# FFN of sub-blocks 1 to 3: the norm's sums of squares behind the first gate step, the spreading of its factors inside the first up step

## The chip, the cores and the metric

The kernel runs on one core of a Trainium2 chip. TensorE (PE, with its weight loads as PEld) multiplies, VectorE (DVE), ScalarE (ACT) and GpSimd (POOL) do the element work, and SyncE (SP) issues the transfers. Each engine works through its own list of instructions in order and waits on semaphores for the others. TensorE writes into PSUM, of which the kernel uses eight tiles of 128 x 512 numbers (called banks here): four for large products (the pool "acc") and four for everything else (the pool "mps").

The metric is the time of one execution on the device, in microseconds. All times below are microseconds.

## The reference

One layer of a hybrid decoder, on 2048 prompt tokens and 8 x 4 sample tokens: a mixer (gated linear attention and a spatial gating unit), attention over 256 memory tokens, and a gated MLP with a causal convolution of width 3 over the tokens. The change touches the way into the last of them:

```
def rmsnorm(x, g):
    xf = x.astype(jnp.float32)
    y = xf * lax.rsqrt(jnp.mean(xf * xf, axis=-1, keepdims=True) + EPS)
    return (y * g.astype(jnp.float32)).astype(x.dtype)

# the MLP, in words:
#   n  = rmsnorm(x, g_ffn)                 1024 columns
#   a  = causal_conv3(n @ w_gate) + bias   2816 columns
#   x += (gelu(a) * (n @ w_up)) @ w_down
```

The factor of the norm is one number for each token, so it can be multiplied in behind the product: `n @ w` is `(x * g) @ w` times that number. The kernel does that: its products start from `x * g`, and the factor comes in later, in g = q x factor (before the convolution) and once more behind the GELU for the up half.

## The kernel before, in words

**Tiling.** The prompt is worked through in four sub-blocks s = 0 to 3 of 512 tokens; in the FFN sub-block 2 also takes the 32 sample tokens (544 columns). Activations lie with features on partitions, tokens along the row. Every float32 product is three passes with rounded halves (`mm3`, lines 92 to 94: high x high, low x high, high x low); a matmul here is one such pass of 128 x 128 weights.

**The FFN.** 2816 columns are 22 tiles of 128, taken in pairs as 11 gate steps and 11 up steps that alternate (gate 0, up 0, gate 1, ...), with down steps woven in later. In sub-block 0 a step is an ordinary product with 512 tokens (`gate`, `upp`). In sub-blocks 1 to 3 it is `gate7` or `upp7`, which share `seven_step`: the 2 x 2 x 2 blocks of a step in seven products (A11, S1, A12, S2, S3, S4, A22) rather than eight, on half the tokens (256, or 272) each, from sums of token blocks (`w1`, `wu`, `wt`, `wb`, made by DVE and ACT for each pair of feature tiles, four pairs) and sums of weight tiles. A product is 4 pairs x 3 passes, 12 matmuls; a step is 84. For gate step 0 (`early`) all seven products first run over the three token pairs that are there, then over the last pair; its products A11, S1, A12 and S2 take the four banks of "acc", S3, S4 and A22 take banks of "mps". When a product is complete, DVE or ACT adds it to the step's result q (lines 266 to 288), and `use` consumes q.

**The norm.** The last product of the attention (`out_proj_steps`, product name wx) calls `finish(m)` for each of the eight feature tiles: ACT squares it, POOL adds the squares up in `wxsq` (line 1265). Two steps follow:

- `stat` (here called xstat, lines 1267 to 1277): matmuls of `wxsq` with a column of ones give the sum for each token in `wxss` (128 x 4, line 1272; a float32 matmul is two passes, so 8 in the profile, 10 in sub-block 2), DVE scales it into `rt` (line 305), POOL raises it to the power -1/2 (`wxrs`, line 306).
- `start` (fstart), that is `bcast_tokens` (lines 308 to 323): DVE makes four diagonal tiles `dg_f` (line 313), four matmuls with ones spread them over all partitions into the bank `bcp_f` (line 314), ACT copies it to `bc_f` (line 316); sub-block 2 has a small fifth one (`bcps_f`, lines 321 and 322).

`bc_f` is first read by the gate step's `use`: `gate_put` (line 1540) makes g = q x bc_f, and `conv` runs the convolution and the GELU.

**What sets the order.** The kernel is written as a list of steps, `x2 + [xstat, fstart] + fmain`, and a scheduler places the instructions of each engine from this list, by its own model of times and by what is free. A step written earlier has its PSUM bank reserved earlier, so wxss and bcp_f take banks of "mps" ahead of S3, S4 and A22 of gate step 0.

Of the kernel before, what the change touches and what calls it, by code (L numbers as in the profile page):

```python
# [37 lines left out]
def hymba_step_kernel(  # L38
# [172 lines left out]
            return wsplit(raw[:, :1024].rearrange("p (k m) -> p k m", k=8), name)  # L211
        return load

    def seven_step(plain, sums, get_xs, H, use, name, early=False):


        seq = ("A11", "S1", "A12", "S2", "S3", "S4", "A22") if early else ("A11", "S2", "S1", "S3", "A12", "S4", "A22")
# [14 lines left out]
        def fn(*ws):  # L232
# [6 lines left out]
            q = wraw(f"q_{name}")  # L239
# [3 lines left out]
            def prod(nm, k0, k1):  # L243
                if nm not in ps:
                    mate = {"S3": "S1", "A22": "S4"}.get(nm)
                    if joint and mate:
                        ps[nm] = ps[mate][0], 1
                    else:
                        ps[nm] = (mps if early and len(ps) > 3 else acc)(f"a_{name}{nm}"), 0
                bank, i = ps[nm]  # L250
                for k in range(k0, k1):
                    mm3(bank[:, i * H:(i + 1) * H], half(nm, 0, k), half(nm, 1, k), *xs[k][nm], k == 0, k == last)
# [9 lines left out]
                    prod(nm, 0, last)  # L262
            for nm in seq:
                prod(nm, last if early else 0, last + 1)
                if nm == "A11":
                    act.activation(q0, got(nm), AF.Copy)
                elif nm == "S2":
# [237 lines left out]
    w7d = {}  # L505
# [1012 lines left out]
    def ffn_steps(B, last=False):  # L1518
# [36 lines left out]
        def gate7(j):  # L1555
            f = 2 * j
            H = T // 2

            def use(*q):
                for i in range(2):  # L1560
                    cur["g", f + i] = gate_tile(f + i)
                    gate_put((dve, pool)[i], f + i, q[i], 0, T)
                    conv(f + i)
            return seven_step(*w7d["g", j], lambda: B.hn, H, use, f"wg{s}{j}", j == 0)

        def conv(f):
# [29 lines left out]
        def upp7(j):  # L1596
            f = 2 * j
            H = T // 2

            def use(*q):  # L1600
                for i in range(2):
                    c = cur[f + i]
                    (dve, pool)[i].tensor_tensor(c[:, :T], q[i], c[:, :T], ALU.mult)  # L1603
                    acts[f + i] = (U(f"acth{s}{f + i}", F32R), U(f"actl{s}{f + i}", F32R))
                    split(acts[f + i][0][:, :T], acts[f + i][1][:, :T], c[:, :T])
            return seven_step(*w7d["u", j], lambda: B.hn, H, use, f"wup{s}{j}")

        def turn_h(j):

# [147 lines left out]
    for s, B in enumerate(blocks):  # L1757
# [18 lines left out]
        steps += w2 + [stat, scales]  # L1776
        steps += weave(sc + x1, (turns[:2], 8, 9), (turns[2:3], 13, 13), (turns[3:], 14, 14))
        fstart, fmain, flast = ffn_steps(B, s == NSB - 1)
        steps += x2 + [xstat, fstart]
        sides = []  # L1780
        if B.mix_sample:
            sides.append((sample_steps(), 1, len(fmain) - 5))
# [46 lines left out]
```

## Time and profile before

| | |
|---|---|
| time, median of 3 runs (lowest, highest) | 2842.79 (2840.3, 2844.05) |
| span of the profiled execution | 2835.0 |
| TensorE busy, share of the span | 2794.4, 99% |
| weight loads busy | 2473.9, 87% |
| DVE, ACT, POOL busy | 1891.3, 1104.5, 575.5 |
| first gate matmul of sub-block 1, 2, 3 | 1120.12, 1810.65, 2476.49 |

The profile is of one execution; times in it count from its start. A row of its timeline gives start, duration, engine, line, operation and tiles (out<-in), with the number of instructions drawn together as x, and in brackets the idle time of the engine just before and what ended it. Tile names lose their numbers where rows are grouped (a_wg30S stands for the sums S1 to S4 of gate step 0 of sub-block 3, a_wg30A for A11, A12, A22). TensorE's durations overlap: the distance from start to start is what a matmul costs.

### The profile page before, as it was taken

What the parts mean: (1) busy time and instruction counts of PE and PEld (TensorE: products, weight loads), DVE (VectorE), ACT (ScalarE), POOL (GpSimd) and SP (SyncE); (2) the same over time, 40 slices, a digit from 0 to 9 for tenths busy, and PEclk for the clock granted to TensorE, in tenths of its full rate; (3) what the DMA queues carried; (4) which work ended last, traced back from release to release, by engine and by line L of the source; (5) the groups of instructions that cost most, each with busy time, mean ns of one, the idle gap of its engine ahead of it and who ended that gap; (6) DMA issues with size and microseconds to landing.
All of it is one profiled execution on the core that took longest, in us unless ns stands there. A gap on an engine that the chain in (4) does not pass through costs nothing.

```text
span 2835.0 us, 47063 instructions
## 1 busy us (share of the span) xinstructions
PE 2794.4 (99%) x17894; PEld 2473.9 (87%) x17894; DVE 1891.3 (67%) x3266; ACT 1104.5 (39%) x1950; POOL 575.5 (20%) x638
## 2 busy tenths in 40 slices
PE   8999999999999999999999999999999999999998
PEld 8888888888888898898888889899999888899997
DVE  6578778777657776655555777766666677665555
ACT  5645544333363354222124445422223545421222
POOL 2002212111111221222220121222221022132222
PEclk9999999999999999999999999999999999999999
DMA  9756589999932255888995226577776323577775
GB/s 306 244 182 219 188 273 340 335 339 333 328 109 77 83 164 196 309 290 290 324 340 169 82 61 208 196 260 256 258 264 215 102 70 133 201 260 273 271 282 177
DMA packets 369687, 638.21 MB, mean 225 GB/s; under 512 B 27370, under 2 KB 238412, under 8 KB 369462
## 3 DMA queue, kind: packets, MB, share of 16 engines
q1 hardware_dynamic: 369462, 635.20, 65.9%
q8 instruction: 142, 2.33, 0.3%
q14 instruction: 83, 0.68, 0.1%
HBM read 507.69 MB, written 127.41 MB: 224 GB/s over the span
## 4 chain that ended last, share of the span: by engine, by line
PE 61%; DVE 4%; ACT 1%; issue 1%; POOL 1%; DMA 0%; POOLq 0%; SPq 0%; DVEq 0%; ACTq 0%
PE d L94 4%; PE d L92 4%; PE d L93 4%; PE a_wx L94 1%; PE a_wx L93 1%; PE a_wx L92 1%; PE s L1044 1%; PE a_wo L92 1%; PE a_wo L93 1%; PE a_wu L92 1%; PE a_wu L93 1%; PE a_wo L94 1%; PE t_wr L92 1%; PE t_wr L93 1%; PE a_wu L94 1%
## 5 line engine op out<-in xcount | busy, mean ns | idle before, releaser
L92 PE MATMUL d<-acth,whi_wd 128*128 128x272 f32 (+1 forms) x688 | 235.3, 342 | 0.0
L94 PE MATMUL d<-acth,wlo_wd 128*128 128x272 f32 (+1 forms) x688 | 233.3, 340 | 0.0
L93 PE MATMUL d<-actl,whi_wd 128*128 128x272 f32 (+1 forms) x688 | 233.0, 339 | 0.0
L1679 DVE TENSOR_TENSOR h<-d,h 128x512 f32<-128x512 f32 (+1 forms) x232 | 133.5, 581 | 148.0 <-PE d L94 147.8
L1581 POOL TENSOR_TENSOR c<-c,bc_f 128x512 f32<-128x512 f32 (+1 forms) x88 | 139.3, 1589 | 134.2 <-ACT c L1580 133.4
L1571 ACT ACTIVATE c<-g,colsb 128x512 f32<-128x512 f32 x88 | 71.7, 815 | 202.9 <-DVE g L1540 152.7
L94 PEld LDWEIGHTS d<-acth,wlo_wd 128*128 128x128 f32 x688 | 129.3, 188 | 15.5 <-issue 1.2
L93 PEld LDWEIGHTS d<-actl,whi_wd 128*128 128x128 f32 x688 | 129.3, 188 | 13.6 <-issue 0.4
L92 PEld LDWEIGHTS d<-acth,whi_wd 128*128 128x128 f32 x688 | 129.5, 188 | 13.1
L1603 POOL TENSOR_TENSOR c<-r_q_wup,c 128x512 f32<-128x512 f32 (+1 forms) x33 | 63.0, 1908 | 337.7 <-DVE r_q_wup L286 215.9
L1568 POOL COPY carry<-g 128x2 f32<-128x2 f32 x88 | 30.6, 348 | 432.8 <-DVE g L1540 430.7
L92 PE MATMUL a_wo<-ch,h_wo 128*128 128x512 f32 (+1 forms) x320 | 113.2, 365 | 2.3 <-ACT r L874 1.5
L93 PE MATMUL a_wo<-cl,h_wo 128*128 128x512 f32 (+1 forms) x320 | 113.4, 357 | 0.0
L94 PE MATMUL a_wo<-ch,l_wo 128*128 128x512 f32 (+1 forms) x320 | 112.6, 355 | 0.0
L1572 DVE SCALAR_TENSOR_TENSOR c<-g,colsb,c 128x512 f32<-128x512 f32 x88 | 86.0, 978 | 29.0 <-ACT c L1571 28.3
L84 ACT ACTIVATE acth<-c 128x512 fp32r<-128x512 f32 (+1 forms) x88 | 55.9, 636 | 117.1 <-DVE c L1603 87.3
L94 PE MATMUL a_wx<-pTh,wlo_wx 128*128 128x512 f32 x256 | 101.2, 395 | 0.0
L93 PE MATMUL a_wx<-pTl,whi_wx 128*128 128x512 f32 x256 | 100.5, 393 | 0.0
L92 PE MATMUL a_wx<-pTh,whi_wx 128*128 128x512 f32 x256 | 100.2, 394 | 0.0
L1580 ACT ACTIVATE c<-c 128x512 f32<-128x512 f32 (+1 forms) x88 | 56.1, 637 | 96.6 <-DVE c L1573 84.7
L1573 DVE SCALAR_TENSOR_TENSOR c<-g,colsb,c 128x512 f32<-128x512 f32 x88 | 88.0, 1000 | 1.1
L85 DVE TENSOR_TENSOR actl<-c,acth 128x512 fp32r<-128x512 f32 (+1 forms) x88 | 64.2, 733 | 27.2 <-ACT acth L84 26.2
(3753 smaller groups left out, 9725.5 us busy)
## 6 DMA issues: line engine op xcount, KB each, us to landing
whi_wd<-wd SPq DMA_DIRECT2D x66, 512.0 KB, 7.8
wlo_wd<-wd SPq DMA_DIRECT2D x66, 512.0 KB, 7.5
r_wo<-in_w_out_dram SPq DMA_DIRECT2D x32, 512.0 KB, 3.5
wlo_wx<-vod SPq DMA_DIRECT2D x32, 512.0 KB, 4.1
whi_wx<-vod SPq DMA_DIRECT2D x32, 512.0 KB, 4.8
r_wg<-in_w_gate_dram SPq DMA_DIRECT2D x22, 512.0 KB, 7.4
r_wup<-in_w_up_dram SPq DMA_DIRECT2D x22, 512.0 KB, 4.7
r_wd<-in_w_down_dram SPq DMA_DIRECT2D x22, 512.0 KB, 4.3
```

What stands on the lines that cost most here:

```text
L84: act.activation(hi, src, AF.Copy)
L85: (lo_eng or dve).tensor_tensor(lo, src, hi.bitcast(F32), ALU.subtract)
L92: pe.matmul(ps, wh, xh, start=first, stop=False)
L93: pe.matmul(ps, wh, xl, start=False, stop=False)
L94: pe.matmul(ps, wl, xh, start=False, stop=last)
L1571: act.activation(c[:, :SB], g[:, 2:SB + 2], AF.Identity, bias=cb, scale=w2)
L1572: dve.scalar_tensor_tensor(c[:, :SB], g[:, 1:SB + 1], w1, c[:, :SB], ALU.mult, ALU.add)
L1573: dve.scalar_tensor_tensor(c[:, :SB], g[:, 0:SB], w0, c[:, :SB], ALU.mult, ALU.add)
L1580: act.activation(c[:, :T], c[:, :T], AF.Gelu_apprx_tanh)
L1581: pool.tensor_tensor(c[:, :T], c[:, :T], B.fbc[:, :T], ALU.mult)
L1603: (dve, pool)[i].tensor_tensor(c[:, :T], q[i], c[:, :T], ALU.mult)
L1679: dve.tensor_tensor(B.h[m + mm][:, cs], ps[:, :cw], B.h[m + mm][:, cs], ALU.add)
```

## The change

For sub-blocks 1 to 3 the two steps leave the list. The first gate step's `use`, called when its seven products have been written, runs xstat in place of its own work and keeps its results q; the first up step gets a function `then`, which `seven_step` calls behind product S1: it runs `start` (the spreading) and then the gate's real `use` with the kept results. Sub-block 0 is as before, since its steps aren't of this form. No instruction is added or taken away.

```diff
--- before.py
+++ after.py
@@ -211,7 +211,7 @@
             return wsplit(raw[:, :1024].rearrange("p (k m) -> p k m", k=8), name)
         return load
 
-    def seven_step(plain, sums, get_xs, H, use, name, early=False):
+    def seven_step(plain, sums, get_xs, H, use, name, early=False, then=None):
 
 
         seq = ("A11", "S1", "A12", "S2", "S3", "S4", "A22") if early else ("A11", "S2", "S1", "S3", "A12", "S4", "A22")
@@ -262,6 +262,8 @@
                     prod(nm, 0, last)
             for nm in seq:
                 prod(nm, last if early else 0, last + 1)
+                if then and nm == "S1":
+                    then()
                 if nm == "A11":
                     act.activation(q0, got(nm), AF.Copy)
                 elif nm == "S2":
@@ -1557,10 +1559,16 @@
             H = T // 2
 
             def use(*q):
+                if j == 0 and "late" not in cur:
+                    B.xstat()
+                    cur["late"] = q
+                    return
                 for i in range(2):
                     cur["g", f + i] = gate_tile(f + i)
                     gate_put((dve, pool)[i], f + i, q[i], 0, T)
                     conv(f + i)
+            if j == 0:
+                cur["use"] = use
             return seven_step(*w7d["g", j], lambda: B.hn, H, use, f"wg{s}{j}", j == 0)
 
         def conv(f):
@@ -1603,7 +1611,12 @@
                     (dve, pool)[i].tensor_tensor(c[:, :T], q[i], c[:, :T], ALU.mult)
                     acts[f + i] = (U(f"acth{s}{f + i}", F32R), U(f"actl{s}{f + i}", F32R))
                     split(acts[f + i][0][:, :T], acts[f + i][1][:, :T], c[:, :T])
-            return seven_step(*w7d["u", j], lambda: B.hn, H, use, f"wup{s}{j}")
+            def then():
+                start()
+                cur.pop("use")(*cur["late"])
+                del cur["late"]
+
+            return seven_step(*w7d["u", j], lambda: B.hn, H, use, f"wup{s}{j}", then=then if j == 0 else None)
 
         def turn_h(j):
 
@@ -1776,7 +1789,8 @@
         steps += w2 + [stat, scales]
         steps += weave(sc + x1, (turns[:2], 8, 9), (turns[2:3], 13, 13), (turns[3:], 14, 14))
         fstart, fmain, flast = ffn_steps(B, s == NSB - 1)
-        steps += x2 + [xstat, fstart]
+        B.xstat = xstat.fn
+        steps += x2 + ([xstat, fstart] if s == 0 else [])
         sides = []
         if B.mix_sample:
             sides.append((sample_steps(), 1, len(fmain) - 5))
```

**TensorE, end of gate step 0 of sub-block 3.** Before (a_wg30S2 is product S2, its operands the token sums wu, the last pair with the number 37; wup30A11 is the up step's first product):

```order
L93 MATMUL a_wg30A11_25852<-w1wx37_25789,wg30A11_25566 128x256
L94 MATMUL a_wg30A11_25852<-w1wx37_25789,wg30A11_25566 128x256
L92 MATMUL a_wg30A12_25872<-wbhwx37_25798,wg30A12_25627 128x256
L93 MATMUL a_wg30A12_25872<-wblwx37_25799,wg30A12_25627 128x256
L94 MATMUL a_wg30A12_25872<-wbhwx37_25798,wg30A12_25627 128x256
L1272 MATMUL wxss3_25811<-ones_86,wxsq3_25525 128x1 x4
L92 MATMUL a_wg30S2_25882<-wuhwx37_25802,wg30S2_25629 128x256
L92 MATMUL a_wup30A11_25988<-w1wx31_25544,wup30A11_25720 128x256
L93 MATMUL a_wup30A11_25988<-w1wx31_25544,wup30A11_25720 128x256
L94 MATMUL a_wup30A11_25988<-w1wx31_25544,wup30A11_25720 128x256
```

And now:

```order
L93 MATMUL a_wg30S4_25878<-wblwx37_25799,wg30S4_25659 128x256
L94 MATMUL a_wg30S4_25878<-wbhwx37_25798,wg30S4_25659 128x256
L93 MATMUL a_wg30S1_25838<-wtlwx37_25794,wg30S1_25568 128x256
L94 MATMUL a_wg30S1_25838<-wthwx37_25793,wg30S1_25568 128x256
L93 MATMUL a_wg30S3_25868<-wtlwx37_25794,wg30S3_25657 128x256
L94 MATMUL a_wg30S3_25868<-wthwx37_25793,wg30S3_25657 128x256
L92 MATMUL a_wg30A22_25888<-wuhwx37_25802,wg30A22_25718 128x256
L93 MATMUL a_wg30A22_25888<-wulwx37_25803,wg30A22_25718 128x256
L94 MATMUL a_wg30A22_25888<-wuhwx37_25802,wg30A22_25718 128x256
L1274 MATMUL wxss3_25927<-ones_86,wxsq3_25525 128x1 x4
L92 MATMUL a_wup30A11_25953<-w1wx31_25544,wup30A11_25720 128x256
L93 MATMUL a_wup30A11_25953<-w1wx31_25544,wup30A11_25720 128x256
```

The sums of squares, which stood where A11 and A12 were complete, S2 and S1 lacked the last pair, and S3, S4 and A22 had not begun, now stand behind the last matmul of the gate step, with the up step right after them.

**TensorE, the spreading in sub-block 3.** Before, the first of the four matmuls (the other three stand together, 16 rows further on, inside S4):

```order
L92 MATMUL a_wg30S1_25862<-wthwx37_25793,wg30S1_25568 128x256
L93 MATMUL a_wg30S1_25862<-wtlwx37_25794,wg30S1_25568 128x256
L94 MATMUL a_wg30S1_25862<-wthwx37_25793,wg30S1_25568 128x256
L314 MATMUL bcp_f3_25820<-dg_f30_25821,ones_86 128x128
L92 MATMUL a_wg30S3_25892<-wthwx31_25548,wg30S3_25657 128x256
L93 MATMUL a_wg30S3_25892<-wtlwx31_25549,wg30S3_25657 128x256
L94 MATMUL a_wg30S3_25892<-wthwx31_25548,wg30S3_25657 128x256
L92 MATMUL a_wg30S3_25892<-wthwx33_25609,wg30S3_25657 128x256
```

And now, all four (a_wup30S1 holds S1 and S3 of the up step in one bank; these rows are the end of S3, and A12 is the product behind it):

```order
L92 MATMUL a_wup30S1_25981<-wthwx35_25700,h_wup30S1_25813 128x256
L93 MATMUL a_wup30S1_25981<-wtlwx35_25701,h_wup30S1_25813 128x256
L94 MATMUL a_wup30S1_25981<-wthwx35_25700,l_wup30S1_25814 128x256
L92 MATMUL a_wup30S1_25981<-wthwx37_25793,h_wup30S1_25813 128x256
L316 MATMUL bcp_f3_25994<-dg_f30_25995,ones_86 128x128
L316 MATMUL bcp_f3_25994<-dg_f31_25998,ones_86 128x128
L93 MATMUL a_wup30S1_25981<-wtlwx37_25794,h_wup30S1_25813 128x256
L94 MATMUL a_wup30S1_25981<-wthwx37_25793,l_wup30S1_25814 128x256
L316 MATMUL bcp_f3_25994<-dg_f32_26001,ones_86 128x128
L316 MATMUL bcp_f3_25994<-dg_f33_26004,ones_86 128x128
L92 MATMUL a_wup30A12_26043<-wbhwx31_25553,wup30A12_25817 128x256
```

The spreading moved from the middle of the gate step to the end of the up step's S3, 46 matmuls behind the sums of squares; the blocks are two and two instead of one and three. In sub-block 1 it stands at the same place, with one small matmul of the sample's projection beside the second block; in sub-block 2 all four stand together inside S3, and the small fifth two matmuls further on.

**VectorE, the same stretch of sub-block 3.** Before (rt is the scaling of the sums, dg_f30 to dg_f33 the diagonals, l_wup30S1 the low half of the up step's weight sum, the lines 258 to 288 the evacuations into q):

```order
L85 TENSOR_TENSOR wulwx37_25803<-t24wx37_25788,wuhwx37_25802 128x512
L305 TENSOR_SCALAR rt_25817<-wxss3_25811 128x4
L85 TENSOR_TENSOR wtlwx37_25794<-t13wx37_25787,wthwx37_25793 128x512
L313 TENSOR_SCALAR dg_f30_25821<-ident_81,wxrs3_25812 128x128
L313 TENSOR_SCALAR dg_f31_25824<-ident_81,wxrs3_25812 128x128
L313 TENSOR_SCALAR dg_f32_25827<-ident_81,wxrs3_25812 128x128
L313 TENSOR_SCALAR dg_f33_25830<-ident_81,wxrs3_25812 128x128
L268 TENSOR_TENSOR r_q_wg30_25851<-a_wg30S2_25882,r_q_wg30_25851 128x256
L258 TENSOR_TENSOR r_q_wg30_25851<-a_wg30A12_25872,r_q_wg30_25851 128x256
L85 TENSOR_TENSOR l_wup30S1_25838<-r_wup30S1_25835,h_wup30S1_25837 128x1024
```

And now:

```order
L279 TENSOR_TENSOR r_q_wg30_25827<-a_wg30S1_25838,r_q_wg30_25827 128x256
L280 TENSOR_TENSOR r_q_wg30_25827<-a_wg30S3_25868,r_q_wg30_25827 128x256
L85 TENSOR_TENSOR l_wup30S1_25814<-r_wup30S1_25811,h_wup30S1_25813 128x1024
L281 TENSOR_TENSOR r_q_wg30_25827<-a_wg30S3_25868,r_q_wg30_25827 128x256
L290 TENSOR_TENSOR r_q_wg30_25827<-a_wg30A22_25888,r_q_wg30_25827 128x256
L307 TENSOR_SCALAR rt_25933<-wxss3_25927 128x4
L285 TENSOR_TENSOR r_q_wg30_25827<-a_wg30S4_25878,r_q_wg30_25827 128x256
L315 TENSOR_SCALAR dg_f30_25995<-ident_81,wxrs3_25928 128x128
L315 TENSOR_SCALAR dg_f31_25998<-ident_81,wxrs3_25928 128x128
L270 TENSOR_TENSOR r_q_wup30_25952<-a_wup30S2_25967,r_q_wup30_25952 128x256
L315 TENSOR_SCALAR dg_f32_26001<-ident_81,wxrs3_25928 128x128
L315 TENSOR_SCALAR dg_f33_26004<-ident_81,wxrs3_25928 128x128
```

The scaling and the diagonals now stand behind the split of the up step's weight sum and the evacuations of the gate step, and among the first evacuations of the up step.

## The prediction

> **What bounds the kernel now.** I read the page first: its span and its busy times.
> ```profile
> span 2835.0 us, 47063 instructions
> PE 2794.4 (99%) x17894; PEld 2473.9 (87%) x17894; DVE 1891.3 (67%) x3266; ACT 1104.5 (39%) x1950; POOL 575.5 (20%) x638
> ```
> TensorE is busy for 99% of the span and no other engine comes near, so only time that TensorE gets back can shorten the kernel. A transfer, a VectorE step or a POOL step counts only where TensorE stands still for it. The profiled span is 2835.0; the median of the three runs is 2842.79, which is 7.8 more. I work out a gain in the span and take it off the median.
>
> Next I read the table by stretches, for the three places that the change touches (from the first gate matmul of sub-blocks 1, 2 and 3 on) and for two undisturbed stretches right behind the last two of them. The columns are the length, then busy time and instructions of PE, PEld, DVE, ACT and POOL, then the granted clock, the DMA share and GB/s.
> ```profile
> 1120.12:1134.84 14.72, 13.86 (x113) 13.39 (x112) 10.97 (x21) 6.26 (x10) 4.37 (x4) 1.00 0.32 109
> 1810.65:1828.17 17.52, 16.80 (x129) 16.03 (x128) 13.60 (x27) 9.83 (x21) 6.12 (x11) 1.00 0.45 153
> 2476.49:2491.20 14.71, 13.84 (x114) 13.38 (x113) 10.97 (x21) 6.27 (x10) 4.35 (x4) 1.00 0.42 145
> 2491.20:2499.67 8.47, 8.47 (x74) 8.47 (x73) 7.41 (x12) 3.75 (x5) 3.50 (x6) 1.00 0.81 258
> 1828.17:1834.18 6.01, 6.01 (x50) 6.01 (x49) 5.81 (x12) 3.54 (x6) 3.76 (x6) 1.00 0.70 239
> ```
> The clock is 1.00 everywhere. What the first three stretches lose shows in the timeline of TensorE, here sub-block 3 (start, duration; the bracket is idle time and what ended it).
> ```profile
> 2482.21 1.05 PE L1272 MATMUL wxss<-ones,wxsq 128*128 128x1 f32 x8 [0.61 <-POOL wxsq L1265]
> ...
> 2485.41 0.28 PE L94 MATMUL a_wg30S<-wthwx,wg30S 128*128 128x256 f32 x1
> 2485.96 0.46 PE L314 MATMUL bcp_f<-dg_f,ones 128*128 128x128 f32 x2 [0.26 <-DVE dg_f L313]
> 2486.17 0.36 PE L92 MATMUL a_wg30S<-wthwx,wg30S 128*128 128x256 f32 x1
> 2486.38 0.27 PE L93 MATMUL a_wg30S<-wtlwx,wg30S 128*128 128x256 f32 x1
> ...
> 2488.04 0.28 PE L92 MATMUL a_wg30S<-wbhwx,wg30S 128*128 128x256 f32 x1
> 2488.16 0.83 PE L314 MATMUL bcp_f<-dg_f,ones 128*128 128x128 f32 x6
> 2488.74 0.37 PE L93 MATMUL a_wg30S<-wblwx,wg30S 128*128 128x256 f32 x1
> 2488.95 0.28 PE L94 MATMUL a_wg30S<-wbhwx,wg30S 128*128 128x256 f32 x1
> ```
> The matmuls' durations overlap, so I count from start to start (the x of a stretch also counts the two that run in over its edge). From 2491.20 to 2499.67 72 matmuls start, **0.1176 each**. From 2476.49 to 2491.20 there are 96 (84 of the gate step, 12 of the up step's A11): 11.29 at that rate, against 14.71. So 3.42 goes to the sums of squares (wxss) and the spreading (bcp_f). In sub-block 1, of the same shapes, it is 14.72 - 11.29 = 3.43. Sub-block 2 has 272 columns and a rate of its own: 48 matmuls in 6.01, 0.1252 each; its stretch holds 108, 13.52 of 17.52, so 4.00 is lost. Together **10.85** is the most that could come back.
>
> That sum goes by the interval. By the busy column the three stretches have only 0.86 + 0.72 + 0.87 = 2.45 to give, and by PEld, the weight loads, 1.33 + 1.49 + 1.33 = 4.15. The Trainium skill, page "Perfetto Trace Analysis", section "Identifying the Most-Contended Engine", says that matmul busy time does not tell how near TensorE is to its limit, because pipelined instructions look otherwise in the trace, and that the weight loads' share should be read. By the first reading the time could at best be 2840.3, by the second 2838.6. The trace agrees with the page: in the undisturbed stretch PEld too is 8.47 of 8.47.
>
> **The change part by part.** The instructions stay the same in kind and number; nothing is loaded that wasn't. What moves is one short chain per sub-block: eight (ten) passes for the sums, one small DVE and one POOL instruction, four DVE diagonals, eight (ten) passes of spreading, one or two ACT copies, and behind them the gate's scaling. None of it issues a DMA.
>
> *The wait for the sums goes.* Now wxss stands after two of the seven products' last pieces and waits 0.61 for POOL; since wxss and bcp_f take PSUM banks ahead of S3, S4 and A22, TensorE can't fill the time with these. In the new order all seven products run first: 63 matmuls from 2476.49 to 2483.90, then the last 21 to 2486.37, then wxss.
> ```profile
> 2480.36 1.79 POOL L1265 TENSOR_TENSOR wxsq<-wxsq,wxq 128x512 f32<-128x512 f32 x1 [2.97 <-ACT wxq L1260]
> 2483.92 0.69 DVE L85 TENSOR_TENSOR wtlwx<-t13wx,wthwx 128x512 fp32r<-128x512 f32 x1
> ```
> POOL's last sum ends at 2482.15, 4.2 before it is needed. The last token piece, wtl, ends at 2484.61; its first use, 15 matmuls into the last 21, comes at about 2485.6. No wait is left, only the passes.
>
> *The price of the passes* I take from sub-block 0, where the same two sets stand inside steady 512-column matmuls (0.23 apart):
> ```profile
> 421.30 0.95 PE L1272 MATMUL wxss<-ones,wxsq 128*128 128x1 f32 x8
> 422.11 0.48 PE L92 MATMUL a_wg<-wxh,h_wg 128*128 128x512 f32 x1
> 422.42 0.39 PE L93 MATMUL a_wg<-wxl,h_wg 128*128 128x512 f32 x1
> ...
> 429.11 1.05 PE L314 MATMUL bcp_f<-dg_f,ones 128*128 128x128 f32 x8
> 429.92 0.48 PE L92 MATMUL a_wup<-wxh,h_wup 128*128 128x512 f32 x1
> 430.23 0.39 PE L93 MATMUL a_wup<-wxl,h_wup 128*128 128x512 f32 x1
> ```
> From the block's start to the second matmul behind it is 1.12 both times; one interval of 0.23 is due, so **0.89 for eight passes in one block**. In the new order the spreading of sub-blocks 1 and 3 stands in two blocks of four passes. Two blocks are in the rows above: two passes cost 2486.38 - 2485.41 less two intervals and less the 0.26 waited, 0.475; six cost 2488.95 - 2488.04 less two intervals, 0.675. That is 0.05 a pass and 0.375 a block, 1.15 for both. So after: 0.89 + 1.15 = 2.04, gains of 1.39 (sub-block 1) and 1.38 (3). Sub-block 2: ten passes of sums 0.89 x 10/8 = 1.11, spreading 0.89 for one block of eight and 0.475 for the sample's two, 2.48 in all; gain 1.52. **Sum 4.29.** From below the price is 0.05 a pass if a block costs nothing to enter (0.80, 0.80 and 1.00 instead of 2.04, 2.04 and 2.48: 3.96 more gain, 8.25); from above it is what it is now, no gain. I take the middle, which is measured on the same instructions.
>
> *The added wait: bcp_f for its diagonals.* What is to hide the chain from the sums to the spreading is the up step's A11, S2, S1 and most of S3.
> ```profile
> 2483.74 0.15 DVE L305 TENSOR_SCALAR rt<-wxss 128x4 f32<-128x4 f32 x1
> 2483.97 1.52 POOL L306 TENSOR_TENSOR wxrs<-rt,neghalf 128x4 f32<-128x4 f32 x1 [1.82 <-DVE rt L305]
> 2485.14 1.06 ACT L84 ACTIVATE h_wup30S<-r_wup30S 128x1024 fp32r<-128x1024 f32 x1 [1.25 <-PE a_wup30A L94]
> 2485.53 0.87 DVE L313 TENSOR_SCALAR dg_f<-ident,wxrs 128x128 f32<-128x128 f32 x4 [0.91 <-POOL wxrs L306]
> 2487.10 1.22 DVE L85 TENSOR_TENSOR l_wup30S<-r_wup30S,h_wup30S 128x1024 fp32r<-128x1024 f32 x1
> 2489.03 0.60 ACT L316 ACTIVATE bc_f<-bcp_f 128x512 f32<-128x512 f32 x1 [2.56 <-PE bcp_f L314]
> 2492.34 0.69 DVE L1540 TENSOR_TENSOR g<-r_q_wg,bc_f 128x512 f32<-128x512 f32 x1
> 2529.39 0.39 PE L92 MATMUL d<-acth,whi_wd 128*128 128x512 f32 x1
> ```
> From rt's start (2483.74) to the first pass of bcp_f (2485.96) is 2.22. In the new order rt waits for wxss (over at 2486.37 + 0.89 = 2487.26) and on VectorE stands behind the split l_wup30S1 and two evacuations of the gate. The split's ACT half can start when gate S2 is done (about 2485.3; it takes 1.06), the split runs from about 2486.9 for 1.22, two additions of 0.35 follow, so rt starts at about 2488.8 and bcp_f may go at 2491.0. TensorE is there after 12 + 12 + 22 more matmuls, 2487.26 + 46 x 0.1176 = 2492.67. **1.65 of cover is left**; each us past rt at 2490.45 is a us of stall, up to three times in the kernel.
>
> *What is late next.* TensorE is through with the spreading at 2492.67 + 1.15 + two matmuls = 2494.06, bc_f takes 0.60 from there, and g comes at about 2494.9 and not 2492.34, while TensorE is 1.4 ahead. Behind g on VectorE stands the evacuation of the up step's A12 (about 2496). Gate step 1 begins at 2476.49 + 168 x 0.1176 + 2.04 = 2498.29 and asks for that bank at its S1, 24 matmuls later, 2501.1. The chain of convolution, GELU and products, later by 2.6, ends in activations that the first down step (2529.39) uses. I cost it at nothing; its cover is 5 at the nearest place.
>
> *The sample's projection* in sub-block 1 also shifts: the product with r_sq21 stands inside the up step 1 now.
> ```profile
> 1152.21 1.22 DVE L85 TENSOR_TENSOR l_wup11S<-r_wup11S,h_wup11S 128x1024 fp32r<-128x1024 f32 x1
> wg12S<-s7g SPq DMA_DIRECT2D x4, 512.0 KB, 9.9
> r_sq<-in_wq_x_dram SPq DMA_DIRECT2D x6, 512.0 KB, 5.9
> 1162.30 0.40 PE L1404 MATMUL sqp<-r_sq,smpx 128*32 128x256 f32 x1
> ```
> TensorE would reach it at about 1162.30 - 1.4 + 0.8 = 1161.7. On SP r_sq21 waits for that split (over at 1153.43), so it goes at about 1153.7 and lands at 1159.6 by its own median of 5.9, but at 1163.6 by the 9.9 of its neighbours: between nothing and 1.9 of stall. I take nothing.
>
> **The rivals.**
> - *The wait only moves* (the change doesn't do what it says). If rt starts 1.4 past 2490.45 in each sub-block, bcp_f stalls for what wxss saved: **2842.8**. For it: the chain through POOL's 1.52 is long, and VectorE is 75% busy there. Against: 1.65 of cover.
> - *Slower: the split of the up step's S1 sum comes late.* Now its ACT half waited for the up step's A11. If that release stays, it starts at 2488.7, the split at 2490.1; at the 2.31 that the same split took elsewhere it ends at 2492.4, and TensorE, which wants it at 2490.3, stands for 2.2. rt then starts at 2493.2, bcp_f could go at 2495.4 against 2494.9: 2.7 in all, 1.3 more than was saved, three times: **2846.7**. It decides from a total stall of 1.4 on, with the shorter split about when ACT starts at 2488.7. Against: the buffer is released by gate S2 in the new order.
> ```profile
> 2501.95 2.31 DVE L85 TENSOR_TENSOR l_wup31S<-r_wup31S,h_wup31S 128x1024 fp32r<-128x1024 f32 x1
> ```
> - *More comes back*: the passes cost only their 0.05: 2842.79 - 8.25 = **2834.5**. For it: the products are free to run around them. Against: sub-block 0 paid 0.89 with nothing waiting.
> - *r_sq21 lands late*: 1.9 of the gain is lost: **2840.4**.
>
> **How the numbers follow.** Forecast 2842.79 - 4.29 = **2838.5** (span 2830.7), chance 0.58; wait moves 0.16; more comes back 0.10; r_sq21 0.10; slower 0.06. The low end is the cheapest passes (2834.5), the high end the moved wait with the before's own upper spread of 1.3 (2844.0). A measurement of this kernel tells about 0.2% from no change, 5.7. The forecast lies inside, 1.4 from the edge at 2837.1. Faster by more takes the cheap passes and part of the forecast's lower side, 0.24; slower by more needs over 2848.5, the slower rival with more on top, 0.05; within 0.2%: 0.71.
>
> **What would show it.** In the profile after: wxss behind the last matmul of A22 without a bracket, the next L93 some 1.1 behind its start; bcp_f in S3 without a bracket; from the first gate matmul to the first matmul of gate step 1 about 21.8 in sub-block 3 (2476.49 to 2499.67, 23.18, now). A bracket on bcp_f from dg_f is the first rival, one on a_wup30S from l_wup30S the second, one on sqp from r_sq the fourth. The prediction is wrong if the stretches shorten as said and the span doesn't: then something downstream took it, to be sought in what TensorE waits for behind 1135, 1828 and 2491.

## The result, and the profile after

| | before | after |
|---|---|---|
| time, median (lowest, highest) of 21 runs each | 2840.44 (2836.81, 2844.05) | 2836.10 (2830.57, 2840.36) |
| ratio of the times, 95% interval | | 0.9985 [0.9979, 0.9991] |
| span of the profiled execution | 2835.0 | 2835.5 |

The time falls by 4.3, or 0.15%: inside the 0.2% that I took for no change, and nearly the number forecast, 4.29. The interval allows for 2.6 to 6.0, so that the medians meet the forecast within 0.1 is chance. The time itself, 2836.10, is 2.4 under the forecast 2838.5, and that is the starting point: the 21 runs of the kernel before have a median of 2840.44, where the three that I had gave 2842.79. The parts of the 4.29 were not all right either, as the stretches show. First the page of the changed kernel: its span and busy times.

```profile
span 2835.5 us, 47052 instructions
PE 2797.1 (99%) x17894; PEld 2477.9 (87%) x17894; DVE 1894.6 (67%) x3266; ACT 1106.0 (39%) x1950; POOL 569.5 (20%) x638
```

**The spans are equal although the median fell by 4.3.** The changed kernel's profiled execution was already 5.8 behind when it came to the change (first gate matmul of sub-block 1 at 1125.90 against 1120.12), though up to there TensorE runs the same instructions in the same order. The table by stretches shows where some of that went (length; busy time and count of PE, PEld, DVE, ACT, POOL; granted clock, DMA share, GB/s). Before:

```profile
287.00:290.00 3.00, 1.30 (x9) 0.73 (x7) 2.06 (x3) 0.22 (x1) 1.63 (x1) 1.00 1.02 371
290.00:295.00 5.00, 4.55 (x20) 3.67 (x20) 2.73 (x4) 2.21 (x4) 0.00 (x0) 1.00 0.63 230
```

And after:

```profile
287.00:290.00 3.00, 0.81 (x6) 0.54 (x6) 2.71 (x5) 0.95 (x2) 1.91 (x1) 0.99 0.96 298
290.00:295.00 5.00, 4.65 (x14) 3.27 (x13) 3.42 (x5) 2.42 (x4) 0.00 (x0) 0.50 0.89 327
```

Here TensorE got half its clock for 5 us, which it didn't before. Such spells fall at a few places of every execution, differently each time. Ahead of the change the two traces have a granted clock of 0.50 from 1028.57 to 1031.98 before, and from 289.94 to 296.77 and 1037.46 to 1044.29 after: 10.2 more at half clock, by my estimate 5.1 of the 5.8. The prediction had named shorter stretches with an equal span as a sign that something downstream took the gain; here the loss lies ahead of the first changed instruction. From there to the end TensorE's waits are those of before without the 1.4 on wxss, the 0.8 on bcp_f and two of 0.5 and 0.3, and one of 0.5 (on a_wo, for ACT) is new. The changed kernel's own times reach from 2830.57 to 2840.36, so one span can't show a gain of 4. Stretches that run at a clock of 1.00 can: in a second profile of the changed kernel they repeat within 0.01. These are the three that the prediction spoke of, each from the first gate matmul of the sub-block to the first matmul of gate step 1. Before:

```profile
1120.12:1144.43 24.31, 23.45 (x201) 22.27 (x199) 19.18 (x34) 10.44 (x15) 8.47 (x11) 1.00 0.59 201
1810.65:1835.83 25.18, 24.46 (x192) 23.69 (x190) 20.95 (x42) 13.86 (x26) 10.97 (x17) 1.00 0.55 189
2476.49:2499.67 23.18, 22.31 (x185) 21.85 (x184) 18.39 (x32) 10.02 (x15) 7.85 (x10) 1.00 0.57 186
```

And after:

```profile
1125.90:1149.45 23.55, 23.55 (x201) 22.27 (x200) 17.29 (x32) 9.40 (x13) 6.09 (x9) 1.00 0.57 205
1813.60:1837.23 23.63, 23.63 (x190) 23.41 (x188) 17.82 (x40) 11.86 (x23) 7.51 (x13) 1.00 0.54 198
2478.56:2500.15 21.59, 21.59 (x185) 21.59 (x184) 15.80 (x30) 8.12 (x12) 6.08 (x9) 1.00 0.53 195
```

TensorE no longer stands: PE is busy for the whole of each. The stretches are shorter by 0.76, 1.55 and 1.59, together **3.90**, where 1.39, 1.52 and 1.38 were predicted. TensorE's timeline of sub-block 3 after the change shows the two blocks (start, duration):

```profile
2488.35 0.28 PE L94 MATMUL a_wg30A<-wuhwx,wg30A 128*128 128x256 f32 x1
2488.47 0.95 PE L1274 MATMUL wxss<-ones,wxsq 128*128 128x1 f32 x8
2489.28 0.37 PE L92 MATMUL a_wup30A<-w1wx,wup30A 128*128 128x256 f32 x1
2489.48 0.28 PE L93 MATMUL a_wup30A<-w1wx,wup30A 128*128 128x256 f32 x1
...
2494.68 0.28 PE L92 MATMUL a_wup30S<-wthwx,h_wup30S 128*128 128x256 f32 x1
2494.79 0.61 PE L316 MATMUL bcp_f<-dg_f,ones 128*128 128x128 f32 x4
2495.15 0.37 PE L93 MATMUL a_wup30S<-wtlwx,h_wup30S 128*128 128x256 f32 x1
2495.35 0.28 PE L94 MATMUL a_wup30S<-wthwx,l_wup30S 128*128 128x256 f32 x1
2495.47 0.61 PE L316 MATMUL bcp_f<-dg_f,ones 128*128 128x128 f32 x4
2495.84 0.37 PE L92 MATMUL a_wup30A<-wbhwx,wup30A 128*128 128x256 f32 x1
2496.04 0.28 PE L93 MATMUL a_wup30A<-wblwx,wup30A 128*128 128x256 f32 x1
```

Both brackets are gone. Counted as in the prediction, from the block's start to the second matmul behind it less one interval, the sums cost 2489.48 - 2488.47 - 0.118 = 0.89 and the two blocks of the spreading 0.44 + 0.45 = 0.89. Sub-block 1 shows what else moved:

```profile
1142.22 0.61 PE L316 MATMUL bcp_f<-dg_f,ones 128*128 128x128 f32 x4
...
1143.00 0.62 PE L1406 MATMUL sqp<-r_sq,smpx 128*32 128x256 f32 x2
...
1143.55 0.71 PE L316 MATMUL bcp_f<-dg_f,ones 128*128 128x128 f32 x4
...
1148.46 1.06 PE L1406 MATMUL sqp<-r_sq,smpx 128*32 128x256 f32 x14
```

Two of the sample projection's 16 passes now stand alone, inside the up step, where before all 16 stood together at 1143.43.

**Where the gain stands at the end of each sub-block.** From the first matmul of gate step 0 to that of gate step 10, sub-blocks 1, 2 and 3 took 338.1, 310.8 and 291.4 before and take 336.2, 310.0 and 289.8 now: 1.9 + 0.8 + 1.6 = 4.3 (in the second profile 336.5, 310.0 and 289.8). Sub-block 3 keeps its gain. Sub-block 2 gives back 0.7: passes that turn the next sub-block's tokens (xt), of which two stood at the end of its stretch before (0.14 of the 1.55 is that they left it), now stand in gate step 1 (one is on record at 1848.12), which takes 0.6 longer. Sub-block 1 loses 0.3 more up to gate step 2 and then wins 1.4. Half of that is the step from gate 2 to up 2 (36.05 before, 35.31 now), where small transposes of the sample stand otherwise; the other half is the sample's attention, where TensorE no longer waits at one place of up step 8, which shrinks from 13.1 to 12.4. Before:

```profile
1425.06 0.64 PE L1495 MATMUL sop<-vc,spm 128*32 128x256 f32 x8
1426.54 0.64 PE L1495 MATMUL sop<-vc,spm 128*32 128x256 f32 x8 [0.52 <-DMA vc<-in_cache_mem_v_dram]
```

### The profile page after: what moved, and what is told of

It reads as the page before. It is cut to its first block, busy times and chain, and to the rows that moved or that the text cites. A ratio compares the mean times of both kernels' runs of the same rounds, so it can differ in the third digit from the quotient of the medians.

```text
span 2835.5 us, 47052 instructions
## 1 busy us (share of the span) xinstructions
PE 2797.1 (99%) x17894; PEld 2477.9 (87%) x17894; DVE 1894.6 (67%) x3266; ACT 1106.0 (39%) x1950; POOL 569.5 (20%) x638
## 3 DMA queue, kind: packets, MB, share of 16 engines
q8 instruction: 142, 2.33, 0.3%
## 4 chain that ended last, share of the span: by engine, by line
PE 63%; DVE 3%; ACT 1%; issue 0%; POOL 0%; DMA 0%; POOLq 0%; DVEq 0%; ACTq 0%
PE d L94 4%; PE d L92 4%; PE d L93 4%; PE a_wx L94 2%; PE a_wx L93 2%; PE a_wx L92 2%; PE a_wo L92 1%; PE s L1046 1%; PE a_wo L93 1%; PE a_wo L94 1%; PE a_wu L92 1%; PE a_wu L93 1%; PE t_wr L92 1%; PE t_wr L93 1%; PE a_wu L94 1%; PE t_wr L94 1%
## 5 line engine op out<-in xcount | busy, mean ns | idle before, releaser
L92 PEld LDWEIGHTS d<-acth,whi_wd 128*128 128x128 f32 x688 | 129.6, 188 | 13.1
```

The costliest lines, as they stand in the source:

```text
L92: pe.matmul(ps, wh, xh, start=first, stop=False)
```

## The experiments

The theory: what comes back is the stop for POOL's last sum (and the small one for the diagonals), in every sub-block, and what remains is the passes. Its rivals: the gain is that of the function `then`; the spreading, not the sums, carries it; or the PSUM banks do. Times of single executions are given for completeness; what is said of these kernels rests on stretches. In sub-block 3 (s3) the stretch is 23.18 before and 21.59 after the change.

**1. Only the sums are moved; the spreading follows at once in the same place of the list.**

```diff
--- after.py
-                if j == 0 and "late" not in cur:
+                if j == 0:
                     B.xstat()
-                    cur["late"] = q
-                    return
+                    start()
...
-            def then():
-                start()
-                cur.pop("use")(*cur["late"])
-                del cur["late"]
```

> The sums of squares behind gate step 0 as in the change, but the spreading and the gate's own use called right there, with no function handed to the up step. In its order the spreading still comes at the end of the up step's S3, in one block of four, and in sub-block 1 the sample's first projection stays in one block. Measure: from the first gate matmul of a sub-block to the first matmul of gate step 1 (before: 24.31 in sub-block 1, 25.14 in 2, 23.18 in 3; changed: 23.55, 23.63, 21.59). Theory (TensorE runs without a stop and pays 0.89 for eight passes; where the spreading is written doesn't matter, since it comes when its factors are ready): 22.7 in sub-block 1, 23.6 in 2, 21.55 in 3. Rival (the place inside the up step is needed, since the spreading would else take a bank early or wait): the stretches stay near those of before, with an idle bracket on bcp_f from dg_f.

Measured: 22.81, 23.63 and 21.60 in sub-blocks 1 to 3, no bracket (2835.64 once, beside 2835.93 for the kernel before). The scheduler puts the spreading behind enough of the up step without being told, here in sub-block 3:

```profile
2493.22 1.05 PE L316 MATMUL bcp_f<-dg_f,ones 128*128 128x128 f32 x8
```

So `then` adds nothing. In sub-block 1 this kernel is 0.74 better than the change. Its order of matmuls there differs from the change's in two things: the spreading is one block and not two, which in sub-block 3 makes 0.01, and the sample's projection stays whole:

```profile
1140.85 1.05 PE L316 MATMUL bcp_f<-dg_f,ones 128*128 128x128 f32 x8
1146.33 1.07 PE L1406 MATMUL sqp<-r_sq,smpx 128*32 128x256 f32 x16
```

**2. Only the spreading is moved.**

```diff
--- after.py
                 if j == 0 and "late" not in cur:
-                    B.xstat()
                     cur["late"] = q
-        steps += x2 + ([xstat, fstart] if s == 0 else [])
+        steps += x2 + ([xstat, fstart] if s == 0 else [xstat])
```

> Half of the change: the sums of squares ahead of the gate step as before, only the spreading inside the up step. Theory (the sums lose 1.98 at the old place, 0.61 of it waiting for POOL, as S4 and A22 can't run for want of a bank; the spreading loses 1.40 there and 0.89 at the new place): sub-block 3 at 19.76 + 1.98 + 0.89 = 22.6, with the bracket of about 0.6 on wxss from POOL still there. Rival (the spreading's place is what counted, the bank of bcp_f held the products back): near 21.6, the bracket on wxss gone or filled.

Measured: 23.96, 24.24 and 22.48 (2840.53 once). The sums wait as before:

```profile
2486.69 1.05 PE L1274 MATMUL wxss<-ones,wxsq 128*128 128x1 f32 x8 [0.61 <-POOL wxsq L1267]
```

In sub-block 3 the move of the spreading is worth 23.18 - 22.48 = 0.70 and that of the sums the other 0.89. Both halves count. In sub-block 1, where 23.96 is only 0.35 less than before, the sample's projection stands in two blocks of eight passes (1146.30 and 1151.33).

**3. Every pass of the sums and of the spreading twice.**

```diff
--- after.py
-            pe.matmul(ps[:, c * 128:(c + 1) * 128], ones, dg[:, :128], start=True, stop=True)
+            for _ in range(2 if name in ("f1", "f2", "f3") else 1):
+                pe.matmul(ps[:, c * 128:(c + 1) * 128], ones, dg[:, :128], start=True, stop=True)
...
+                for _ in range(2 if name == "wx" and s else 1):
+                    pe.matmul(ps[:n, c:c + 1], B.sq[:, c * 128:c * 128 + n], ones[:, 0:1], start=True, stop=True)
```

> The changed kernel with each matmul of the sums and of the spreading issued twice, in sub-blocks 1 to 3: 16 passes more in each. Theory (a pass costs a weight load, about 0.11, wherever it stands): sub-block 3 at 21.59 + 1.78 = 23.4, TensorE without brackets. Rival of the prediction's lower bound (0.05 a pass, the rest is the entry into a block): 21.59 + 0.80 = 22.4. Second rival (they hide behind other work): 21.6.

Measured: 23.38 in sub-block 3 (2844.46 once). Sixteen passes more cost 23.38 - 21.59 = 1.79, **0.11 a pass**. The Trainium skill, page "TensorE: Matmul & The Clock Gate", section "LDWEIGHTS (loading the stationary operand)", gives a weight load as its number of columns divided by 1.2, in ns: 107 for 128 columns. The run agrees: a pass of this kind costs about its weight load. In sub-block 1 the stretch is 24.57, only 1.02 more than the change's, because here the sample's projection stays whole (16 passes at 1150.35); beside kernel 1, where it does too, it is 1.76 more, 0.11 a pass again. Sub-block 2 took 26.99, and not for the passes alone:

```profile
1827.91:1830.00 2.09, 2.09 (x23) 2.06 (x21) 2.09 (x5) 1.22 (x4) 0.00 (x0) 1.00 0.82 227
1830.00:1832.00 2.00, 2.00 (x10) 2.00 (x11) 1.27 (x7) 0.00 (x0) 1.61 (x3) 0.57 0.97 291
1832.00:1834.00 2.00, 2.00 (x12) 2.00 (x11) 0.46 (x3) 1.24 (x4) 0.16 (x1) 0.58 1.02 416
```

The clock falls right behind the twenty passes of the sums (from 1827.91 on), without any idle time that the profile shows. It is 0.50 in every half us from 1830.5 to 1833.5; the 0.57 and 0.58 are means of stretches that reach over the ends of this spell.

**4. The kernel before, without the last of the eight squares in the sums of sub-blocks 1 to 3**, so that POOL is done earlier (the factors are then of seven eighths of the features).

```diff
--- before.py
-                pool.tensor_tensor(B.sq[:, :T], B.sq[:, :T], t[:, :T], ALU.add)
+                if not (name == "wx" and s and m == 7):
+                    pool.tensor_tensor(B.sq[:, :T], B.sq[:, :T], t[:, :T], ALU.add)
```

> The kernel before, with the last of the eight squares left out of the sums in sub-blocks 1 to 3, so that the sums of squares need not wait for POOL's last addition (the factors are then of seven eighths of the features). Theory (the wait shown from POOL is only the last of several: with S3, S4 and A22 held back TensorE would next wait for the last token pieces from ACT and DVE): the bracket on wxss goes, one of 0.3 to 0.8 on a_wg30S from wuhwx or wthwx comes, sub-block 3 at 22.4 to 22.9. Rival (POOL's addition is the cause): all brackets go and sub-block 3 comes to 21.6 as in the changed kernel.

Measured: 23.14, 24.07 and 21.96, no brackets (2832.23 once). The new wait that I expected didn't come, since the scheduler also put the sums earlier, ahead of the last token pair:

```profile
2476.43 0.95 PE L1273 MATMUL wxss<-ones,wxsq 128*128 128x1 f32 x8
```

With POOL's last addition gone, 23.18 - 21.96 = 1.22 of the change's 1.59 come back, with the two steps where they stood in the list. My number fell (22.4 to 22.9); that POOL's lateness is the cause stands firmer for it.

**5. A slow chain: the factor's DVE and POOL steps run three more times**, between the sums and the spreading.

```diff
--- after.py
             rstd_of(rs[:, :4], ps[:, :4], 128, 4, 1.0 / D)
...
+            for _ in range(3 if name == "wx" and s else 0):
+                rstd_of(rs[:, :4], ps[:, :4], 128, 4, 1.0 / D)
```

> The changed kernel with the scaling and the power of the sums (rt and wxrs) computed four times over instead of once in sub-blocks 1 to 3, the same result each time: the chain from the sums to the diagonals is some 3 to 4.5 longer. Its order has the spreading 31 matmuls later, at the end of the up step. Theory (TensorE has other products to run and the chain is covered; what comes late next, g and the evacuations behind it on VectorE, has a cover of 5): sub-block 3 near 21.6 to gate step 1, no bracket on bcp_f, and from there to gate step 2 19.8 as now. Rival (the cover is used up): a bracket on bcp_f from dg_f, or on the products of gate step 1 from the evacuations in lines 258 to 290, of 1 or more in each sub-block.

Measured: 21.59 in sub-block 3, no bracket (2837.37 once). The scheduler knows the longer chain and puts the spreading 31 matmuls later:

```profile
2498.61 1.05 PE L316 MATMUL bcp_f<-dg_f,ones 128*128 128x128 f32 x8
```

Up to gate step 2, sub-block 3 takes 41.4 as after the change: there the chain lies beside TensorE's work, even four times over. Not so in sub-block 1. Its stretch is 22.80, without a wait (the sample's projection is whole here too), but in gate step 1 the rival comes true: ACT comes late to the evacuation that frees a bank, and TensorE stands for it:

```profile
1157.28 0.39 PE L92 MATMUL a_wg11S<-wbhwx,wg11S 128*128 128x256 f32 x1 [1.03 <-ACT r_q_wg L268]
```

Up to gate step 2 sub-block 1 takes 47.6 where kernel 1 takes 47.0, and up to gate step 10 337.8 against the change's 336.2. Sub-block 2 loses 0.6 up to gate step 2 (46.1 against 45.5) without a wait in the profile. So the wait for the diagonals stays away, because the spreading is placed later, but g and the evacuations behind it come later too, and with a chain this long their cover is used up in sub-block 1.

**6 and 7. The change again, and kernel 1, both timed** beside the same runs of the kernel before (2840.11, 27 runs).

> The changed kernel once more, beside the two that follow. If the stretches are what they are for the order's sake, they repeat: 23.55, 23.63 and 21.59, within 0.05, wherever the span comes out. If the runs' spread comes from the granted clock, its profile shows stretches under 1.00 behind the places where TensorE waits, in another number or length than before. Ratio to before 0.9985.

> The kernel of sums_only, timed. By its stretches up to gate step 2 (47.0, 45.5, 41.4 against 48.2, 46.3 and 43.0 before and 47.7, 45.5 and 41.4 changed) it should gain 3.6 to 4.5 on before and 0.7 on the changed kernel: ratio 0.9983 to before. If the place inside the up step had a use that the stretches don't show, it comes out slower than the changed kernel by more than the interval.

Measured: 2836.53, 0.9986 [0.9978, 0.9995] for the change; 2837.56, 0.9989 [0.998, 0.9998] for kernel 1 (11 runs each). The change's result repeats. Kernel 1's 0.74 is there in its stretches, which repeat, but the medians point the other way by 1.0 and both intervals are some 5 us wide: whether it is the better kernel stays open.

**8. One block in place of two**: the sums' weights are the ones, so that a single 512-column matmul (two passes) already spreads them over all partitions, and DVE and ACT turn it into the factor (scale, logarithm, exponential of -0.5 times it). No diagonals, no second block.

```diff
--- after.py
+            if name == "wx" and s:
+                ...
+                    pe.matmul(ps[:, :c1 - c0], ones, B.sq[:, c0:c1], start=True, stop=True)
+                    dve.tensor_scalar(t[:, :c1 - c0], ps[:, :c1 - c0], 1.0 / D, EPS, ALU.mult, ALU.add)
+                    act.activation(t[:, :c1 - c0], t[:, :c1 - c0], AF.Ln)
+                    act.activation(B.fbc[:, c0:c1], t[:, :c1 - c0], AF.Exp, scale=-0.5)
+                return
```

> As sums_only, but the sums are made with the ones as weights, so that they come out spread over all partitions at once (one matmul of 512 columns, two passes, and a small one for the sample), and the factors are exp(-ln/2) on ACT; the diagonals, the spreading and POOL's power are gone in sub-blocks 1 to 3. Theory (what is left of the two steps is the price of 16 weight loads, 1.78): two passes of 512 columns take between 0.5 and 1.1, so sub-block 3 comes to 20.3 to 20.9 against 21.60, and the time is another 2 to 4 under sums_only, ratio 0.997. Rival (ACT's change of tables, 1.28 each, and the work on 512 columns make g late and TensorE waits for the evacuations of gate step 0 or up step 0): brackets of 1 or more in gate step 1, no gain.

Measured: 2834.35, 0.9982 [0.9973, 0.9991] (11 runs); 22.58, 24.75 and 20.66. Sub-block 3 is 0.93 better than the change. Sub-block 1's 22.58 is hardly better than kernel 1's 22.81, since the sample's projection stands in two blocks again:

```profile
1141.80 1.05 PE L1415 MATMUL sqp<-r_sq,smpx 128*32 128x256 f32 x10
...
1147.24 0.63 PE L1415 MATMUL sqp<-r_sq,smpx 128*32 128x256 f32 x6
```

Sub-block 2 is worse, for a transfer of weights that now lands too late (and TensorE stands for 0.5 more in gate step 1, for an evacuation by DVE):

```profile
1832.39 0.37 PE L92 MATMUL a_wup20A<-wbhwx,wup20A 128*128 128x272 f32 x1 [1.58 <-DMA wup20A<-w7u]
```

**9. The kernel before, with the spreading in the bank of the sums**, so that one bank more is free for S3, S4 and A22.

```diff
--- before.py
-        ps = mps(f"bcp_{name}")
+        ps = mps(f"bcp_{name}") if ps is None else ps
...
-            B.fbc = bcast_tokens(B.rs, sample, f"f{s}")
+            B.fbc = bcast_tokens(B.rs, sample, f"f{s}", B.ps if s else None)
```

> The kernel before, but the spreading is written into the bank of the sums, so that the two steps hold one bank of the small pool instead of two; the steps stand where they stood. In its order the sums still come where A11 and A12 are complete, now followed at once by S3, S4 and A22, which find banks; the spreading is one block of four inside S3's end. Theory as the runs so far leave it (TensorE takes its list in order, so a sum that is placed ahead of POOL's last addition stops it whatever else could run behind): the bracket of about 0.6 on wxss stays, none on bcp_f, sub-block 3 at 19.76 + 1.98 + 0.89 = 22.6. Rival, the prediction's own (for want of banks TensorE could not fill the wait): the bracket goes and sub-block 3 comes to 21.6 to 21.9.

Measured: 23.66 and 22.45 in sub-blocks 1 and 3 (2842.02 once). The bank doesn't help the sums; only the bracket of the spreading goes:

```profile
2483.60 0.28 PE L92 MATMUL a_wg30S<-wthwx,wg30S 128*128 128x256 f32 x1
...
2487.38 0.28 PE L94 MATMUL a_wg30A<-wbhwx,wg30A 128*128 128x256 f32 x1
2488.26 1.05 PE L1272 MATMUL wxss<-ones,wxsq 128*128 128x1 f32 x8 [0.61 <-POOL wxsq L1265]
2489.18 0.37 PE L92 MATMUL a_wg30S<-wthwx,wg30S 128*128 128x256 f32 x1
2489.38 0.28 PE L93 MATMUL a_wg30S<-wtlwx,wg30S 128*128 128x256 f32 x1
...
2493.38 1.05 PE L314 MATMUL wxss<-dg_f,ones 128*128 128x128 f32 x8
```

With the bank, the matmul at 2489.18 begins 18 of S3 and S4 that stand right behind the sums; their token sums, wth and wbh, have been in use since 2483.60 and 2484.67, the transfers of their weights were issued by 2471.8 (the one whose landing is on record took 4.1), and the last tile that the small pool held before them, pT, was last read at 2447.3. They could have filled the gap, and wait in the list.

In sub-block 2 this run took 26.3, with a granted clock of 0.79 and 0.90 in places, so it isn't read.

**10. The single block in sub-blocks 1 and 3 only, kernel 1 in sub-block 2** (experiment 8's edit with `if name == "wx" and s in (1, 3)`).

> one_block in sub-blocks 1 and 3, sums_only in sub-block 2, where one_block waited 1.58 for a weight tile. Theory (what one_block lost in sub-block 2 was that wait, which came with the shifted transfers): 22.58, 23.63 and 20.66 to gate step 1, so 5.4 less than before in these three stretches, ratio 0.998 or below. Rival (a transfer comes late elsewhere instead): a bracket from a DMA of 1 or more in sub-block 2 or 3.

Measured: 2835.32 beside 2839.27 for the kernel before (11 and 15 runs), 0.9986 [0.9977, 0.9995]; 22.57, 23.64 and 20.65, no wait in the three stretches. They are 72.67 - 66.86 = 5.8 shorter than before, against 3.9 for the change (the 5.4 that I expected was a slip: my own three numbers make 5.8). The time doesn't tell it from the change.

## Why the prediction was right, and where only its sum was

**The interval method.** It was right: the after's stretches are their matmuls at 0.1176 (0.1252 in sub-block 2) plus the blocks. In sub-block 3, 168 x 0.1176 = 19.76, and 21.59 - 19.76 = 1.83 are left, of which the two blocks are 0.89 + 0.89. The busy column's 2.45 was too little to explain 3.90, as the prediction had it; the 4.15 of the weight loads were enough.

**The wait for the sums goes.** Shown, by experiments 1, 2 and 4. What a stop costs can now be read from the rows of before. Around the sums' block in sub-block 3 stood, before:

```profile
2481.32 0.28 PE L94 MATMUL a_wg30A<-wbhwx,wg30A 128*128 128x256 f32 x1
...
2483.65 0.29 PE L93 MATMUL a_wup30A<-w1wx,wup30A 128*128 128x256 f32 x1
```

The second of these is the third matmul behind the block: 2.33 less three intervals is 1.98 for the block with its stop. Without the stop it costs 0.89, so 1.09 went with a bracket of 0.61. Not all of this is the stop's: in experiment 9, with the same bracket, 2489.38 - 2487.38 less two intervals is 1.76, so the stop costs 0.87, its bracket and 0.26. The other 0.2 lies in the two intervals behind the first matmul after the block: 0.27 and 0.23 in the kernel before, where one matmul of S2 stands alone ahead of the up step, 0.20 and 0.12 in experiment 9. Why they are longer wasn't tried. The spreading's first two passes cost 0.735 with their bracket of 0.26. Experiment 4 has the same two passes without a stop:

```profile
2479.76 0.28 PE L94 MATMUL a_wg30S<-wuhwx,wg30S 128*128 128x256 f32 x1
2479.88 0.41 PE L314 MATMUL bcp_f<-dg_f,ones 128*128 128x128 f32 x2
...
2480.25 0.28 PE L93 MATMUL a_wg30S<-wtlwx,wg30S 128*128 128x256 f32 x1
```

That is 0.49 less two intervals, 0.25. So here too a stop costs its bracket and about 0.25 more.

**Why TensorE stood there.** The step that failed: "since wxss and bcp_f take PSUM banks ahead of S3, S4 and A22, TensorE can't fill the time with these". One bank more (experiment 9) left the stop at 0.61 with matmuls right behind it for which all that the rows show was ready. TensorE works through its list in order, and the sums stood in it ahead of that work. Why the scheduler put them there, presumably since its model has POOL done earlier than the chip, is an inference; shown is that the block moves with POOL's work (experiment 4) and that the bank doesn't decide.

**The price of eight passes in one block**, 0.89 from sub-block 0: measured 0.89.

**Two blocks of four passes**, put at 1.15 by 0.05 a pass and 0.375 a block: mis-sized, measured 0.89, and 0.11 a pass. Splitting costs nothing here. The 0.375 came from a block that began with a stop, of which I had taken off the bracket alone. In sub-block 3 that is why 1.38 became 1.59. In sub-block 2, without such a split, 1.52 became 1.55, with the 0.14 of the passes that left the stretch in it.

**Sub-block 1**, put at 1.39: mis-sized, measured 0.76. The prediction treated its sample passes as a matter of one transfer, and missed that they are also TensorE's own: two of 16 now stand alone, and this costs 0.74 (experiment 1, where they stay together and the stretch is 22.81). Without that split the gain would have been 1.50. The other kernels bear it out. Where the 16 stay together, sub-block 1's stretch is 1.13 to 1.21 longer than sub-block 3's (before, and experiments 1, 3, 4, 5 and 9); cut into 2 and 14 it is 1.96 longer (the change), into 10 and 6 1.92 (experiments 8 and 10), into 8 and 8 1.48 (experiment 2).

**What came back later** was put at nothing and is +0.4 in sum: 1.1 won in sub-block 1, 0.7 given back in sub-block 2. So the forecast's 4.29 and the measured 4.3 agree because errors cancel, which is luck: 0.6 less in sub-block 1's stretch, 0.2 more in the others', 0.4 more behind them.

**The chain and its cover.** The prediction had rt start at 2488.8 and 1.65 of cover. These are the rows after, where all is 2.07 later by the start of the stretch:

```profile
2487.37 1.06 ACT L84 ACTIVATE h_wup30S<-r_wup30S 128x1024 fp32r<-128x1024 f32 x1 [0.45 <-PE a_wg30S L94]
2488.90 1.22 DVE L85 TENSOR_TENSOR l_wup30S<-r_wup30S,h_wup30S 128x1024 fp32r<-128x1024 f32 x1
2490.70 0.15 DVE L307 TENSOR_SCALAR rt<-wxss 128x4 f32<-128x4 f32 x1
2490.93 1.02 POOL L308 TENSOR_TENSOR wxrs<-rt,neghalf 128x4 f32<-128x4 f32 x1 [6.69 <-DVE rt L307]
2491.98 0.48 DVE L315 TENSOR_SCALAR dg_f<-ident,wxrs 128x128 f32<-128x128 f32 x2 [0.80 <-POOL wxrs L308]
2496.12 0.60 ACT L318 ACTIVATE bc_f<-bcp_f 128x512 f32<-128x512 f32 x1 [4.74 <-PE bcp_f L316]
2496.75 0.69 DVE L1542 TENSOR_TENSOR g<-r_q_wg,bc_f 128x512 f32<-128x512 f32 x1
```

rt starts at 2490.70, 2488.63 by the old clock: right to 0.2. The first diagonals are there at about 2492.4 and bcp_f comes at 2494.79, so the cover was 2.4; POOL's step took 1.02 and not 1.52. The split's ACT half is released by the gate's S2, as I had chosen, and not by the up step's A11, so the slower rival had no ground. g comes at 2496.75 (2494.7 by the old clock, against 2494.9) and delays nothing.

**r_sq21** didn't land late: its passes carry no bracket (16 of them at 1167.63). The rival that the passes cost only 0.05 fell with experiment 3. With the two passes at 0.25 (experiment 4) in place of 0.475, the prediction's own split of the rows of before gives 0.105 a pass and nearly nothing a block.

**The 7.8 between span and median** isn't a constant, as the prediction used it. In all 21 runs of the changed kernel the time is 1.7 more than the span of the same execution (2837.18 and 2835.5 for the profiled one). By that the profiled execution of before took about 2836.7, an estimate, and was a quick one. The difference of medians was still well forecast, since the gain was counted in stretches; the span of 2830.7 wasn't.

## What to carry to other kernels

A small product that waits for a late engine, put ahead of work that is ready, costs TensorE its idle time and about 0.25 more for each stop: put it behind the ready work, and its passes, at 0.11 each, are all that is left. Before moving such a step, list the small blocks that other work has in the same stretch, since the scheduler moves those too and one split block gave away 0.74 of a gain of 1.50. A gain of 0.15% is read from stretches at full clock, which repeat to 0.01, and not from the span of one execution.

## What the runs showed of the hardware

- Spells of half the granted clock come and go between executions of one kernel. At 290 us the clock was 0.50 for 5 us behind a stretch in which TensorE was busy for 0.81 of 3.00 and stood for 1.25 at the longest, and 1.00 behind the same stretch with 1.30 of 3.00. In experiment 3 it was 0.50 from 1830.5 to 1833.5 with no idle time at all in the records, behind twenty passes of one column each. The Trainium skill, page "TensorE: Matmul & The Clock Gate", section "What's actually happening", has two states, full and half clock, and the half one after an idle window of some 3.4 us. The two states agree with these rows. The idle window doesn't: the stops ahead of the two spells were 1.25 and none.
- The passes of the 32-column projection cost by the block. From the last matmul ahead of a block to the second behind it, blocks of 16 (before), 14 (the change) and 10 (experiment 8) all take 1.41 to 1.43, and blocks of 8 (experiment 2) and 6 (experiment 8) take 1.00 and 0.99. So the fourteen that were left cost as much as the sixteen before, and two set apart cost 0.74 on top. Splitting the spreading's block of eight cost nothing. What makes the difference wasn't tried.
